# FoX queries and keys computed token-major and turned through DVE squares and DRAM, with the heads queued later

## The chip, the cores and the metric

The kernel runs on one core of one Trainium2 chip. The metric is the device time of one execution in microseconds; the time before is the median of 3 runs. The profile is one further execution, recorded by the hardware profiler. PE is the matrix engine (PEld its weight loads), DVE the vector engine, ACT the scalar engine, POOL and SP the two others, which here mostly issue DMAs.

## The reference

Two layers over 256 tokens of width 2048, each an adaLN-modulated norm, a mixer, a gated residual, then a norm, a SwiGLU FFN of width 5632 and a gated residual. Layer 0 mixes with an mLSTM, layer 1 with FoX attention, 16 heads of 128, which is where the change lies:

```python
def fox_mixer(h, w_in, b_f, w_out):
    proj = h @ w_in
    q, k, v, fl = jnp.split(proj, [D_MODEL, 2 * D_MODEL, 3 * D_MODEL], axis=-1)
    ...
    log_f = jax.nn.log_sigmoid(fl + b_f).transpose(0, 2, 1)
    o = forgetting_attention(heads(q), heads(k), heads(v), log_f)   # causal softmax, bias cum[t] - cum[s]
    return o.transpose(0, 2, 1, 3).reshape(B, T, D_MODEL) @ w_out
```

All is float32.

## The kernel before

**Products.** Float32 accuracy comes from split operands: each operand is kept as a high part (fp32r) and a low part (the remainder), and three products are summed: high by high, high by low, low by high. Weights are read by SP as tiles of four k-tiles by 512 columns, 1 MB each (`fetch`, line 250, from a pool of 5 buffers named raw). `split` (line 255) makes hi on ACT (line 261) and lo on DVE (line 262), two k-tiles at a time, in a pool of 4 pairs, so two weight tiles ahead at most. The normed activations hT (and y, the heads' outputs) hold high and low parts side by side, 512 wide for 256 tokens.

**Two forms of a projection.** `group_a` (line 316) has the activations as stationary and the weights as moving operand: per k-tile, for each of 2 token tiles, three matmuls of 512 columns (lines 288 to 290). It fills 2 PSUM banks with tokens in the partitions (token-major). `group_b` (line 296) has the weights as stationary operand: per k-tile, for each of 4 column tiles, a matmul of 512 moving columns (high weights by both parts of hT, line 271) and one of 256 (low weights by the high part, line 274). It fills 4 banks with columns in the partitions, as the heads want q and k; `total` (line 366) adds the two halves of a bank by an ACT copy and a DVE add. PSUM has 6 banks for projections and 2 (aux) for all else.

**Column steps.** After each weight tile a projection calls `tick` (line 245): it runs the next `adv` pieces of the list `steps`, makes waiting gate rows, and then adds `bgn` of credit for background work. Each whole credit issues one tile of the adaLN modulation (`ada_tile`, line 189): a 1 MB load on SP into the same raw buffers and one DVE instruction of 2.29 us on it. In FoX the credit is 0.66 a step. A clean step is 24 matmuls in `group_a`, 32 in `group_b`. `drain()` with no count runs all that is left in `steps` at once.

**The FoX stage** (lines 1276 to 1306). The first 512 columns of v come first, then the gates, then a loop over i = 0 to 3: q for heads 4i to 4i+3 (512 columns, four steps), k for the same, `drain()`, and then the twelve pieces of these four heads go into `steps`, interleaved over four: four `scores`, four `flip`, four `mix`. `scores` makes the logits on PE (lines 691, 696, 1229), the maximum on DVE (1239), the exponential on ACT (1244), the reciprocal and the scaling of the weights on DVE (1248, 1251). `flip` turns them on PE (958) and copies them (959). `mix` multiplies by v (1261, 1264) and splits the result into y (377, 378). The third value group is finished at i = 1, the fourth is made at i = 2 with two pieces a step; q and k run one piece a step. `project_out` (line 1093) multiplies y by the output weights in three groups of 512 columns and hands the fourth to `bridge`, which begins the FFN; the last four heads run two pieces a step in its first three steps, and the rest of them in a drain ahead of k-tile 12.

**The turn that exists.** The FFN already turns token-major data without PE for some of its groups: `blocks` (line 352) transposes 32x32 squares of a 128x512 tile on DVE (line 353) and writes the tile to a DRAM buffer named aside by POOL's DMA queue (line 357); `gather` (line 359) reads it back in four DMAs (line 361), so that columns stand in the partitions, with the four column tiles innermost; a strided ACT instruction (line 1171) makes it contiguous.

The program is written with a framework that lays out each engine's order and its waits at compile time, following the order of the code; SBUF buffers come from pools (16 slots of 4 KB a partition hold q, k, v, y and the heads' buffers).

Of the kernel before, what the change touches and what calls it, by code (L numbers as in the profile page):

```python
# [9 lines left out]
F32 = mybir.dt.float32  # L10
F32R = mybir.dt.float32r
BF16 = mybir.dt.bfloat16
AF = mybir.ActivationFunctionType
ALU = mybir.AluOpType
# [3 lines left out]
P = 128  # L18
T = 256
D = 2048  # L20
KT = D // P
# [10 lines left out]
def kernel(  # L32
# [5 lines left out]
    nc = tc.nc  # L38
# [13 lines left out]
    def nm(s):  # L52
        n_name[0] += 1
        return f"{s}_{n_name[0]}"

    def slot(dt=F32):
        return slots.tile([P, 1024], dt, tag="slot", name=nm("slot"))

    def bank():
        return psum.tile([P, 512], F32, tag="mm", name=nm("mm"))  # L60
# [4 lines left out]
    def t512():  # L65
        return tmp.tile([P, 512], F32, tag="t512", name=nm("t512"))

    def t256():
        return t512()[:, :T]
# [59 lines left out]
    for i, row in enumerate((crow, crow2)):  # L129
        for j in range(2):  # L130
            ps = bank()
# [100 lines left out]
    steps = []  # L232
# [6 lines left out]
    def drain(n=None):  # L239
        if steps:  # L240
            settle()
        for _ in range(len(steps) if n is None else min(n, len(steps))):
            steps.pop(0)()

    def tick(n, adv=1):
        drain(adv)
        grow_all()
        bg(n)
# [16 lines left out]
    def load_w(w, k0, nk, c0):  # L265
        raw = fetch(w, k0, nk, c0)
        return [p for j in range(0, nk, 2) for p in split(raw, j)]

    def mm_b(ps, hi, lo, rhs, first, last):
        def big():  # L270
            nc.tensor.matmul(ps, hi, rhs, start=first, stop=last, skip_group_check=True)  # L271

        def little():
            nc.tensor.matmul(  # L274
                ps[:, T:], lo, rhs[:, :T], start=False, stop=False, skip_group_check=True
            )

        if last:
            little()
            big()  # L280
        else:
            big()
            little()

    def mm_t(ps, hi, lo, act, t, first, last):
        a = act[:, t * P : (t + 1) * P]
        b = act[:, T + t * P : T + (t + 1) * P]
# [4 lines left out]
    def mm_a(ps, hi, lo, act, first, last):  # L292
        for t in range(2):
            mm_t(ps[t], hi, lo, act, t, first, last)

    def group_b(w, nk, c0, act, evac, bgn, adv=1):
        banks = [bank() for _ in range(4)]
        for k in range(0, nk, 4):
            ws = load_w(w, k, 4, c0)
            for m in range(4):  # L300
                cols = slice(m * P, (m + 1) * P)
                for j, (hi, lo) in enumerate(ws):
                    mm_b(
                        banks[m], hi[:, cols], lo[:, cols], act(k + j), k + j == 0, k + j == nk - 1
                    )
                if k + 4 == nk:
                    evac(m, banks[m])
            tick(bgn, adv)

    late = []  # L310

# [4 lines left out]
    def group_a(  # L316
        w, c0, act, bgn, adv=1, ka=0, kb=KT, row0=0, seed=None, banks=None, before=None, each=None,
        more=False,
    ):
        begun = banks is not None or seed is not None  # L320
        if banks is None:
            banks = [bank() for _ in range(2)]
        if seed is not None:
            for t in range(2):
                nc.scalar.copy(banks[t], seed[:, t, :])
        for k in range(ka, kb, 4):
            if before:
                before(k)
            ws = load_w(w, row0 + k, 4, c0)
            flush()  # L330
            if each:
                each(k)
            for j, (hi, lo) in enumerate(ws):
                mm_a(banks, hi, lo, act(k + j), not begun and k + j == ka, k + j == kb - 1 and not more)
            tick(bgn, adv)
        return banks
# [22 lines left out]
    def gather(whole, aside):  # L359
        for j in range(4):  # L360
            nc.gpsimd.dma_start(
                whole[32 * j : 32 * j + 32].rearrange("a (g b) m -> a g (b m)", b=32),
                aside.rearrange("t (i a) c -> a (t i) c", a=32)[:, :, j * P : (j + 1) * P],
            )

    def total(ps, out, scale=None):
        b = t256()
        nc.scalar.activation(b, ps[:, T:], AF.Copy, scale=1.0 if scale is None else scale)
        if scale is None:
            nc.vector.tensor_tensor(out, ps[:, :T], b, op=ALU.add)  # L370
        else:
            nc.vector.scalar_tensor_tensor(
                out=out, in0=ps[:, :T], scalar=scale, in1=b, op0=ALU.mult, op1=ALU.add
            )

    def split_act(src, dst):
# [365 lines left out]
    w = w_in  # L742
# [205 lines left out]
    def act_tile(lst, k):  # L948
        return lst[k // 2][:, k % 2, :]
# [101 lines left out]
    def interleave(*lists):  # L1051
        return [f for fs in zip(*lists) for f in fs]

    def keep_t(c0, bgn, scale=None, adv=1, layer_w=0):
        if layer_w == 0:
            i = COLS.index(c0)
            unit(i, start[i], KT, bgn)
            sp = SP[i]
            o = slot().rearrange("p (k t) -> p k t", t=T)

            def flip():
                for i in range(2):
                    nc.scalar.copy(o[:, 2 * i : 2 * i + 2, :], turned(sp, i))

            steps.append(flip)
            return o
        o = slot().rearrange("p (k t) -> p k t", t=T)
        group_b(w, KT, c0, h_act, lambda m, ps: total(ps, o[:, m, :], scale), bgn, adv)
        return o

    for i in range(1, 4):
# [20 lines left out]

    def project_out(wo, res, bgn, adv, upto, norm, w2, heads):
        act = lambda k: act_tile(y, k)
        for i in range(3):
            res.both(i, group_a(
                wo, 512 * i, act, bgn, adv, before=lambda k: drain() if k >= upto else None
            ))
        return bridge(wo, 0, KT, 1536, act, res, 3, norm, w2, heads)

# [118 lines left out]
    vals = {}  # L1219

    def fox_head(hd, q, k):
        st = {}

        def scores():
            S = abank()
            logits(u3, hd, S, False)
            for t in range(2):
                n = P * (t + 1)
                nc.tensor.matmul(  # L1229
                    S[:, T * t : T * t + n], q[:, t * P : (t + 1) * P], k[:, :n],  # L1230
                    start=False, stop=t == 1, skip_group_check=True,
                )
            mx = small([P, 2], "den", bufs=4)
            buf = slot()
            W = buf[:, : 3 * P]
            st["W"], st["WT"] = W, buf[:, 512 : 512 + 3 * P]
            sm = small([P, 2], "r", bufs=4)
            for t in range(2):
                nc.vector.tensor_reduce(
                    out=mx[:, t : t + 1], in_=S[:, slice(*causal[t])], axis=AX.X, op=ALU.max,  # L1240
                    negate=True,
                )
            for t in range(2):
                nc.scalar.activation(
                    W[:, slice(*packed[t])], S[:, slice(*causal[t])], AF.Exp,
                    bias=mx[:, t : t + 1], accum_out=sm[:, t : t + 1],
                )
            nc.vector.reciprocal(sm, sm)
            for t in range(2):
                wt = W[:, slice(*packed[t])]  # L1250
                nc.vector.tensor_scalar(wt, wt, sm[:, t : t + 1], None, op0=ALU.mult)

        def flip():
            weights_t(st["W"], st["WT"])

        def mix():
            v, WT = vals[hd // 4][:, :, hd % 4 * P : (hd % 4 + 1) * P], st["WT"]
            if hd % 2 == 0:
                y[hd // 2] = new_act()
            O = abank()  # L1260
            nc.tensor.matmul(
                O[:, :T], v[:, 0, :], WT[:, :T], start=True, stop=False, skip_group_check=True
            )
            nc.tensor.matmul(
                O[:, P:T], v[:, 1, :], WT[:, T:], start=False, stop=True, skip_group_check=True
            )
            split_act(O[:, :T], act_tile(y, hd))

        return [scores, flip, mix]

    def keep_v(banks):
        v = pair(slot())
        copy_a(v, banks)
        return v
# [17 lines left out]
    u3 = split3(cum, 16, new)  # L1292
    for i in range(4):
        if i == 1:
            vals[2] = keep_v(group_a(w, 2 * D + 1024, h_act, FR, ka=12, banks=begun[2 * D + 1024]))
        if i == 2:
            vals[3] = keep_v(group_a(w, 2 * D + 1536, h_act, FR, 2))
        q = keep_t(512 * i, FR, P ** -0.5, layer_w=1)
        k = keep_t(D + 512 * i, FR, layer_w=1)
        drain()  # L1300
        steps.extend(interleave(*[
            fox_head(4 * i + j, q[:, j, :], k[:, j, :]) for j in range(4)
        ]))
    res = Residual(1, G1, True)
    norm = Norm(res, 1, SC2, SH2)
    begun = project_out(fox_out, res, FR, 2, 12, norm, gate_up[1], [0, DFF, 512])
# [116 lines left out]
```

## Time and profile before

| what | value |
|---|---|
| median of 3 runs | 2279.05 us (2278.52 to 2279.84) |
| the profiled execution | 2279.4 us, span 2277.6 us |
| PE, DVE, ACT, POOL busy | 99%, 73%, 50%, 3% |
| granted TensorE clock | 0.999 |
| DMA | 640.69 MB, mean 281 GB/s |

A row of a group gives line, engine, operation, tiles (out<-in), count, then busy time and mean ns of one, then the idle time ahead of it and what ended that. A row of windows gives for a stretch the busy time of each engine with its count of instructions in brackets, then the granted clock, the busy share of the DMA engines and GB/s. A row of the timeline gives start, duration, engine, line and operation; rows of the same kind are merged (x2), and the idle time before the row stands in square brackets. A matmul's end is modelled and reaches into the next, so its pace is the distance between starts.

### The profile page before, as it was taken

The page shows a single profiled execution, that of the slowest core. Times are in us where ns is not written, and L with a number is a line of the kernel's source. Part 1 is how long each engine was busy: PE and PEld are TensorE (multiplying, and loading weights), DVE is VectorE, ACT ScalarE, POOL GpSimd, SP SyncE. Part 2 cuts the span into 40 slices and gives each one's busy share as a digit, 9 for nine tenths or more (in the row PEclk, how much of TensorE's full clock was granted, in tenths as well). Part 3 has the DMA queues.
Part 4 walks back from the last instruction along what each step waited for, and adds up shares of the span by engine and source line. Part 5 has one row for each costly group of instructions (what it writes and reads, how often), then busy time and mean ns, then how long its engine had stood idle before and what let it go on. Part 6 is the DMA issues. An engine that isn't in the chain of part 4 may idle for free.

```text
span 2277.6 us, 26530 instructions
## 1 busy us (share of the span) xinstructions
PE 2255.0 (99%) x10250; PEld 1848.2 (81%) x10250; DVE 1653.0 (73%) x1865; ACT 1139.6 (50%) x1493; POOL 71.2 (3%) x136
## 2 busy tenths in 40 slices
PE   8999999999999999999999999999999999999998
PEld 5877878888888888888888888887888888888886
DVE  7998789878887878875687777777665555555564
ACT  4778564555543344444555444455444443444443
POOL 1000000000000000100000000000100100010000
PEclk9999999999999999999999999999999999999999
DMA  9998989788888889996667877675777665566662
GB/s 394 371 369 321 353 307 354 283 338 334 325 335 330 326 335 349 360 350 219 217 238 288 299 273 277 250 274 189 271 276 255 221 204 189 201 223 219 206 233 98
DMA packets 93571, 640.69 MB, mean 281 GB/s; under 512 B 11443, under 2 KB 11891, under 8 KB 19077
## 3 DMA queue, kind: packets, MB, share of 16 engines
q1 hardware_dynamic: 86400, 617.79, 73.5%
q0 software_dynamic: 6896, 21.08, 3.1%
q8 instruction: 80, 1.31, 0.2%
q14 instruction: 47, 0.38, 0.0%
q10 hardware_dynamic: 148, 0.14, 0.0%
HBM read 628.44 MB, written 10.52 MB: 281 GB/s over the span
## 4 chain that ended last, share of the span: by engine, by line
PE 87%; DVE 5%; DMA 4%; ACT 2%; issue 1%; POOL 0%; SPq 0%; ACTq 0%; DVEq 0%; POOLq 0%
PE mm L289 25%; PE mm L290 25%; PE mm L288 25%; PE mm L271 5%; PE mm L274 3%; DMA ada<-in_ada_w_dram 3%; DVE lo L262 2%; DVE ada L193 2%; ACT hi L261 1%; DMA slot<-in_w_in_dram 1%; PE aux L1010 0%; PE aux L498 0%; PE aux L1229 0%; PE mm L569 0%; PE mm L565 0%
## 5 line engine op out<-in xcount | busy, mean ns | idle before, releaser
L262 DVE TENSOR_TENSOR lo<-raw,hi 128x1024 fp32r<-128x1024 f32 x764 | 924.2, 1221 | 470.8 <-ACT hi L261 469.5
L261 ACT CAST hi<-raw 128x1024 fp32r<-128x1024 f32 x764 | 796.9, 1054 | 870.7 <-PE mm L290 742.2
L289 PE MATMUL mm<-lo,hT 128*128 128x512 f32 x1846 | 720.3, 390 | 3.3 <-DVE lo L262 3.2
L290 PE MATMUL mm<-hi,hT 128*128 128x512 f32 x1846 | 719.8, 390 | 0.0
L288 PE MATMUL mm<-hi,hT 128*128 128x512 f32 x1846 | 719.1, 392 | 0.0
L193 DVE SCALAR_TENSOR_TENSOR ada<-ada,cs 128x2048 f32<-128x2048 f32 x192 | 438.7, 2285 | 55.7 <-DMA ada<-in_ada_w_dram 55.3
L289 PEld LDWEIGHTS mm<-lo,hT 128*128 128x128 f32 x1846 | 346.7, 188 | 78.5 <-DVE lo L262 7.4
L290 PEld LDWEIGHTS mm<-hi,hT 128*128 128x128 f32 x1846 | 346.5, 188 | 72.4 <-issue 0.5
L288 PEld LDWEIGHTS mm<-hi,hT 128*128 128x128 f32 x1846 | 346.5, 188 | 71.9 <-issue 0.5
L288 PE MATMUL mm<-hi,slot 128*128 128x512 f32 x960 | 375.0, 391 | 0.2 <-ACT slot L1043 0.2
L289 PE MATMUL mm<-lo,slot 128*128 128x512 f32 x960 | 374.2, 390 | 0.2 <-DVE lo L262 0.2
L290 PE MATMUL mm<-hi,slot 128*128 128x512 f32 x960 | 374.1, 390 | 0.0
L288 PEld LDWEIGHTS mm<-hi,slot 128*128 128x128 f32 x960 | 180.3, 188 | 38.0 <-ACT slot L1043 0.8
L290 PEld LDWEIGHTS mm<-hi,slot 128*128 128x128 f32 x960 | 180.2, 188 | 37.7 <-issue 0.7
L289 PEld LDWEIGHTS mm<-lo,slot 128*128 128x128 f32 x960 | 180.2, 188 | 37.5 <-DVE lo L262 0.6
L271 PE MATMUL mm<-hT,hi 128*128 128x512 f32 x512 | 181.5, 401 | 0.0
L274 PE MATMUL mm<-hT,lo 128*128 128x256 f32 x512 | 138.4, 281 | 0.4 <-DVE lo L262 0.4
L271 PEld LDWEIGHTS mm<-hT,hi 128*128 128x128 f32 x512 | 94.4, 188 | 19.6
L274 PEld LDWEIGHTS mm<-hT,lo 128*128 128x128 f32 x512 | 96.6, 189 | 4.1 <-DVE lo L262 1.1
L865 ACT ACTIVATE slot<-mm 128x512 f32<-128x512 f32 x78 | 45.3, 596 | 39.7 <-PE mm L290 37.9
L357 POOL DMA_DIRECT2D aside<-t x32 | 18.0, 562 | 1239.7 <-DVE t L353 1239.7
L1172 DVE TENSOR_TENSOR slot<-slot,slot 128x512 fp32r<-128x512 f32 x32 | 34.8, 1090 | 24.8 <-ACT slot L1171 24.8
(220 smaller groups left out, 1049.6 us busy)
## 6 DMA issues: line engine op xcount, KB each, us to landing
ada<-in_ada_w_dram SPq DMA_DIRECT2D x192, 1024.0 KB, 6.3
raw<-in_gate_up_dram SPq DMA_DIRECT2D x176, 1024.0 KB, 5.2
raw<-in_down_dram SPq DMA_DIRECT2D x88, 1024.0 KB, 4.9
raw<-in_fox_in_dram SPq DMA_DIRECT2D x48, 1024.0 KB, 4.9
raw<-in_w_in_dram SPq DMA_DIRECT2D x44, 1024.0 KB, 7.2
raw<-in_w_out_dram SPq DMA_DIRECT2D x16, 1024.0 KB, 5.8
raw<-in_fox_out_dram SPq DMA_DIRECT2D x16, 1024.0 KB, 4.9
aside<-t POOLq DMA_DIRECT2D x32, 256.0 KB, 2.5
```

What stands on the lines that cost most here:

```text
L193: nc.vector.scalar_tensor_tensor(out=raw, in0=raw, scalar=1.0, in1=cs, op0=ALU.mult, op1=ALU.mult, accum_out=acc[layer][:, j : j + 1],)
L261: nc.scalar.copy(hi, raw[:, j : j + 2, :])
L262: nc.vector.tensor_tensor(lo, raw[:, j : j + 2, :], hi.bitcast(F32), op=ALU.subtract)
L271: nc.tensor.matmul(ps, hi, rhs, start=first, stop=last, skip_group_check=True)
L274: nc.tensor.matmul(ps[:, T:], lo, rhs[:, :T], start=False, stop=False, skip_group_check=True)
L288: nc.tensor.matmul(ps, a, hi, start=first, stop=False, skip_group_check=True)
L289: nc.tensor.matmul(ps, a, lo, start=False, stop=False, skip_group_check=True)
L290: nc.tensor.matmul(ps, b, hi, start=False, stop=last, skip_group_check=True)
L357: nc.gpsimd.dma_start(aside, dst)
L865: nc.scalar.activation(SP[i][:, t, :], banks[t], func)
L1172: nc.vector.tensor_tensor(dst[:, :, T:], ps, dst[:, :, :T].bitcast(F32), op=ALU.subtract)
```

## The change

`group_b`, `mm_b` and `total` go. A FoX q or k group is now computed by `group_a`, evicted by two ACT copies (with the scale for q), turned by `blocks` and `gather`, and made contiguous by one ACT copy of 128x1024. A counter of steps, `clock`, is added, and a list `timed`, whose entries `tick` runs when their step has come: the contiguous copy five steps after its group (four for the last k), and the queueing of a block of heads one step after the copy of its k. The twelve pieces of a block are interleaved in two pairs (scores, scores, flip, flip, mix, mix, and again), two a step everywhere. The fourth value group moves behind the last k. `project_out` does the first 12 k-tiles of its first two groups ahead of the drain, and their last four after it.

```diff
     def tick(n, adv=1):
+        clock[0] += 1
+        while timed and timed[0][0] <= clock[0]:
+            timed.pop(0)[1]()
         drain(adv)
...
-        o = slot().rearrange("p (k t) -> p k t", t=T)
-        group_b(w, KT, c0, h_act, lambda m, ps: total(ps, o[:, m, :], scale), bgn, adv)
+        banks = group_a(w, c0, h_act, bgn, adv)
+        whole = slot().rearrange("p (t m) -> p t m", m=4)
+        aside = dram.tile([2, P, 512], F32, tag="aside", name=nm("aside"))
+        for t in range(2):
+            own = t512()
+            nc.scalar.activation(own, banks[t], AF.Copy, scale=1.0 if scale is None else scale)
+            blocks(t512(), own, aside[t])
+        gather(whole, aside)
+        o = slot().rearrange("p (m t) -> p m t", t=T)
+        timed.append((
+            clock[0] + LAND, lambda: nc.scalar.copy(o, whole.rearrange("p t m -> p m t"))
+        ))
         return o
...
         act = lambda k: act_tile(y, k)
+        first = {}
+        if upto == 12:
+            for i in range(2):
+                first[i] = group_a(wo, 512 * i, act, bgn, adv, kb=upto, more=True)
+            assert not timed
+            drain()
         for i in range(3):
             res.both(i, group_a(
-                wo, 512 * i, act, bgn, adv, before=lambda k: drain() if k >= upto else None
+                wo, 512 * i, act, bgn, adv, ka=upto if i in first else 0, banks=first.get(i),
+                before=lambda k: drain() if k >= upto else None,
             ))
...
     for i in range(4):
         if i == 1:
-            vals[2] = keep_v(group_a(w, 2 * D + 1024, h_act, FR, ka=12, banks=begun[2 * D + 1024]))
-        if i == 2:
-            vals[3] = keep_v(group_a(w, 2 * D + 1536, h_act, FR, 2))
-        q = keep_t(512 * i, FR, P ** -0.5, layer_w=1)
-        k = keep_t(D + 512 * i, FR, layer_w=1)
-        drain()
-        steps.extend(interleave(*[
-            fox_head(4 * i + j, q[:, j, :], k[:, j, :]) for j in range(4)
-        ]))
+            vals[2] = keep_v(
+                group_a(w, 2 * D + 1024, h_act, FR, 2, ka=12, banks=begun[2 * D + 1024])
+            )
+        q = keep_t(512 * i, FR, P ** -0.5, 2, layer_w=1)
+        if i == 3:
+            LAND = 4
+        k = keep_t(D + 512 * i, FR, None, 2, layer_w=1)
+        heads = [fox_head(4 * i + j, q[:, j, :], k[:, j, :]) for j in range(4)]
+        timed.append((clock[0] + LAND + 1, lambda hs=heads: steps.extend(
+            interleave(*hs[:2]) + interleave(*hs[2:])
+        )))
+    vals[3] = keep_v(group_a(w, 2 * D + 1536, h_act, FR, 2))
```

More of the change, by code (lines that the diff above doesn't have):

```diff
@@ L243, in drain @@
             steps.pop(0)()
+    clock = [0]
+    timed = []
     def tick(n, adv=1):
+        clock[0] += 1
+        while timed and timed[0][0] <= clock[0]:
+            timed.pop(0)[1]()
         drain(adv)
@@ L267, in load_w @@
         return [p for j in range(0, nk, 2) for p in split(raw, j)]
[L269 to L283, printed above, removed]
     def mm_t(ps, hi, lo, act, t, first, last):
@@ L294, in mm_a @@
             mm_t(ps[t], hi, lo, act, t, first, last)
[L296 to L308, printed above, removed]
     late = []
@@ L363, in gather @@
                 aside.rearrange("t (i a) c -> a (t i) c", a=32)[:, :, j * P : (j + 1) * P],
[L364 to L373, printed above, removed]
             )
@@ L1052, in interleave @@
         return [f for fs in zip(*lists) for f in fs]
+    LAND = 5
     def keep_t(c0, bgn, scale=None, adv=1, layer_w=0):
```

## The prediction

> **What bounds the kernel now.** I read the page first (busy shares, chain, costliest groups), then windows over the FoX stage, then PE's timeline in that stage.
>
> ```profile
> span 2277.6 us, 26530 instructions
> ...
> PE 2255.0 (99%) x10250; PEld 1848.2 (81%) x10250; DVE 1653.0 (73%) x1865; ACT 1139.6 (50%) x1493; POOL 71.2 (3%) x136
> ...
> PE 87%; DVE 5%; DMA 4%; ACT 2%; issue 1%; POOL 0%; SPq 0%; ACTq 0%; DVEq 0%; POOLq 0%
> ...
> L271 PE MATMUL mm<-hT,hi 128*128 128x512 f32 x512 | 181.5, 401 | 0.0
> ...
> L274 PE MATMUL mm<-hT,lo 128*128 128x256 f32 x512 | 138.4, 281 | 0.4 <-DVE lo L262 0.4
> ```
>
> PE is busy 99% of the span and makes 87% of the chain that ended last, so only shorter PE work, or a PE stall gained or lost, moves the time. The change deletes L271 and L274: 1024 matmuls, all of the q and k projections of FoX. Their busy times overlap, because matmuls are pipelined, so what they cost must be read from start to start. I cut the stage into column steps, each a weight tile of four k-tiles by 512 columns.
>
> ```profile
> core 0: us, PE busy (x) PEld busy (x) DVE busy (x) ACT busy (x) POOL busy (x), PEclk, DMA share, GB/s
> ...
> 1215.15:1261.23 46.08, 45.65 (x258) 39.19 (x256) 34.37 (x45) 23.02 (x32) 0.00 (x0) 1.00 0.73 270
> 1371.51:1399.84 28.33, 28.33 (x164) 24.48 (x162) 20.84 (x24) 11.40 (x16) 0.00 (x0) 1.00 0.80 287
> 1267.49:1273.23 5.74, 5.74 (x34) 4.94 (x33) 3.69 (x8) 4.21 (x9) 0.00 (x0) 1.00 1.01 400
> 1293.21:1298.85 5.64, 5.64 (x36) 4.95 (x35) 4.11 (x6) 2.39 (x5) 0.00 (x0) 1.00 0.85 289
> 1352.62:1358.36 5.74, 5.74 (x36) 4.99 (x35) 3.96 (x4) 1.71 (x3) 0.00 (x0) 1.00 0.97 388
> ```
>
> The first window is q and k of i = 0: 8 steps of 32 matmuls (x258 counts neighbours that reach over the edges), no head beside them. The second is 5 such steps. The last three are one step each: the first after a score, then after a flip, then after a mix. The form to come already runs in this stage for the value columns:
>
> ```profile
> start us, us, engine line op out<-in xcount [idle before <-releaser]
> ...
> 1326.64 0.58 PE L288 MATMUL mm<-hi,hT 128*128 128x512 f32 x1
> ...
> 1327.52 0.39 PE L288 MATMUL mm<-hi,hT 128*128 128x512 f32 x1
> ...
> 1331.60 0.39 PE L288 MATMUL mm<-hi,hT 128*128 128x512 f32 x1
> ...
> 1332.28 0.39 PE L691 MATMUL aux<-u,sel 96*128 96x512 bf16 x1
> ...
> 1340.30 0.48 PE L288 MATMUL mm<-hi,hT 128*128 128x512 f32 x1
> ...
> 1345.84 0.82 PE L958 MATMUL aux<-ident,slot 128*128 128x128 f32 x6
> ```
>
> From 1327.52 to 1331.60 lie 18 matmuls, 0.2267 us each, so a clean step of 24 takes 5.44 us. The step after scores takes 5.64 (1326.64 to 1332.28), the one after flips 5.54 (1340.30 to 1345.84).
>
> **The change, part by part. The projections.** Per k-tile the old form streams four times 512 + 256 columns in 8 matmuls, the new one six times 512 in 6: the same 3072 columns, a quarter fewer instructions. Without a head the old step takes (46.08 + 28.33 - 0.75) / 13 = 5.67 us; the 0.75 is a stall treated next. Against 5.44 this is 0.23 saved, 13 times: 3.0 us. Beside heads the rows give 5.74 against 5.64 after a score and 5.64 against 5.54 after a flip, so 0.10; after a mix I have only the old 5.74 and estimate 0.2. Over the 19 steps beside heads that is about 2.3 us. Sum 5.3 us less; bounds 4.4 (0.1 on half of the 13 steps too) and 6.0. The heads' own matmuls, 48 pieces, stay as they are and only move.
>
> By rows an instruction therefore costs a fixed part besides its columns: a pair of 512 and 256 takes 5.67 / 16 = 0.354 us (0.349 beside heads, 5.58 / 16), so 256 columns take 0.122 to 0.127, and twice that less 0.2267 leaves 0.018 to 0.028 us; times 256 fewer matmuls, 4.6 to 7 us, which agrees with the sum. [...]
>
> **The one stall of the old steps.**
>
> ```profile
> 1246.24 2.29 DVE L193 SCALAR_TENSOR_TENSOR ada<-ada,cs 128x2048 f32<-128x2048 f32 x1 [3.62 <-DMA ada<-in_ada_w_dram]
> ...
> 1249.06 0.40 PE L271 MATMUL mm<-hT,hi 128*128 128x512 f32 x1
> 1249.73 0.39 PE L274 MATMUL mm<-hT,lo 128*128 128x256 f32 x1 [0.27 <-DVE lo L262]
> ```
>
> DVE stood 3.62 us before a background ada tile that had not landed; lo came late behind it; PE lost 0.67 - 0.24 = 0.43 here and some 0.3 at the next pair. Nothing in the change removes this, so I count 0, with a bound of 0.75 gained.
>
> **Evictions and the turn.**
>
> ```profile
> L865 ACT ACTIVATE slot<-mm 128x512 f32<-128x512 f32 x78 | 45.3, 596 | 39.7 <-PE mm L290 37.9
> ...
> L1171 ACT CAST slot<-slot 128x512 fp32r<-128x512 f32 x32 | 35.7, 1118 | 19.9 <-DMA slot<-aside 19.9
> ...
> L353 DVE STREAM_TRANSPOSE t<-slot 128x512 f32<-128x512 f32 x32 | 31.8, 1066 | 0.0
> ...
> L368 ACT ACTIVATE t<-mm 128x256 f32<-128x256 f32 x32 | 12.2, 383 | 17.5 <-PE mm L271 17.5
> ...
> L370 DVE TENSOR_TENSOR slot<-mm,t 128x256 f32<-128x256 f32 x16 | 6.5, 419 | 2.5 <-ACT t L368 2.5
> L372 DVE SCALAR_TENSOR_TENSOR slot<-mm,t 128x256 f32<-128x256 f32 x16 | 6.4, 417 | 0.9 <-ACT t L368 0.7
> ```
>
> Removed: 12.2 us on ACT, 12.9 on DVE. Added on ACT: 16 evictions of 596 ns, and 8 strided copies of 128x1024, which I take as two of L1171, 2.24 us each: 27.4 us. Added on DVE: 16 transposes of 1066 ns, 17.1 us. So ACT gets 15 us more and DVE 4 us, none of it on PE's path as long as hi and lo come in time. What the cover is worth:
>
> ```profile
> 880.00:1000.00 120.00, 119.93 (x529) 98.80 (x528) 103.56 (x100) 55.16 (x56) 8.07 (x14) 1.00 0.97 364
> ...
> 1216.00:1444.00 228.00, 227.56 (x1278) 195.03 (x1277) 171.97 (x240) 110.10 (x185) 0.00 (x0) 1.00 0.77 280
> ```
>
> FoX would go from 172 to 176 us of DVE and from 110 to 125 of ACT in some 223 us: 79% and 56%. In 880 to 1000, layer 0's FFN, the same transposes and trips through DRAM run with DVE at 86%, DMA share 0.97, 364 GB/s, and PE is busy 119.93 of 120. So I count 0. If that cover were gone, each us that lo is late on all 32 steps would cost as many us.
>
> **The trip and its waits.** Each of the 8 groups writes 2 x 256 KB and reads 4 x 128 KB on POOL's queue, which is empty in this stage (x0). SP's queue gets nothing new; it only finds the engines fuller. The gather waits on POOL for the write; the copy waits on ACT for the gather, and behind the copy stand the hi casts and the heads' exps, for which DVE's lo and then PE wait.
>
> ```profile
> 908.03 2.00 DVE L353 STREAM_TRANSPOSE t<-slot 128x512 f32<-128x512 f32 x2
> ...
> 916.46 1.76 POOL L361 DMA_DIRECT2D slot<-aside  x3 [5.57 <-DMA aside<-t]
> ...
> 929.18 1.12 ACT L1171 CAST slot<-slot 128x512 fp32r<-128x512 f32 x1
> ```
>
> In the FFN the turned data is used 21.2 us after the first transpose. Here the copy is queued five steps after its group, 5 x 5.44 = 27.2 us or more, and for the last k four steps, 21.8 us and the heads between them. I count 0; the bounds are 0 and the rival below. The copy's own 2.24 us delays a hi cast, which has two steps of hi and lo buffers ahead of it.
>
> **The heads.** The changed schedule runs two pieces a step in pairs: a pair's flips come one step after its scores, where before they came two steps after. The chain scores, max, exp, reciprocal, scale must end within that step.
>
> ```profile
> 1332.19 0.54 DVE L1251 TENSOR_SCALAR slot<-slot,r 128x128 f32<-128x128 f32 x2
> ...
> 1340.64 0.54 DVE L1251 TENSOR_SCALAR slot<-slot,r 128x128 f32<-128x128 f32 x2
> ```
>
> The score pieces that end at 1326.64 would have flips at 1326.64 + 5.44 = 1332.1; their second head is scaled at 1332.7, 0.6 late. Those that end at 1334.08 would have them at 1339.5 and are scaled at 1341.2, 1.7 late, behind another ada tile. Bounds for 8 pairs: 0 (other matmuls are put ahead of the flips) and 8 x 1.15 = 9 us. I take 0.9, near zero: all that PE waited for from 1180 to 1560 is two lines, and L1251 is not among them, although the heads' pieces follow L1251 there too.
>
> ```profile
> PE aux L498 <- DVE slot L487: 1.6, 1, 1.6
> PE mm L274 <- DVE lo L262: 0.4, 2, 0.3
> ```
>
> Drains in one block go:
>
> ```profile
> 1470.06 0.47 PE L289 MATMUL mm<-lo,slot 128*128 128x512 f32 x1
> 1470.49 0.70 PE L1261 MATMUL aux<-slot,slot 128*128 128x256 f32 x2
> ```
>
> Here a mix stood behind its flip's copy, 0.43 - 0.23 = 0.2 us. The new order spreads the last heads over ten steps: 0.2 gained, bound 0.6. The value columns and the first 12 k-tiles of two output groups only change places, with their weight loads on SP; the number of steps, and so of background tiles, is the same.
>
> **Sum.** -5.3 + 0 + 0 - 0.2 + 0.9 = -4.6 us. The profiled execution took 2279.4 us, span 2277.6 and 1.8 around it: 2274.8. The median of the runs, 2279.05, is 0.35 below the profiled one, so 2274.5.
>
> **The rivals.**
>
> *A larger gain.* The projections reach 6.0, the 0.75 stall is not met again, the block drain gives 0.6, the flips cost nothing: 7.3, so 2271.7. For it: PE's waits are down to those two lines. Chance 0.15.
>
> *Part of it given back.* DVE meets unlanded ada tiles more often, since 8 MB more move in a stage that has no-head steps as short as the FFN's, and flips wait: 3 to 4 us lost, 2277.5 to 2278.5, no change that can be told. For it: the stall at 1249 at only 270 GB/s, and the 1.7 above. Against: PE at 119.93 of 120 in the FFN. Chance 0.22.
>
> *The fixed price per matmul is not what is saved.* [...] Against: 0.2267 at 1327 to 1331 in the same stage. Chance 0.07.
>
> *Slower: the gather lands after the copy is reached.* ACT then stands in front of the hi casts. The FFN's 21.2 us leave 6 us to the five steps, and the buffers ahead some 5 more, so it decides from landings about 11 us later than in the FFN; at 13 us, each of 8 copies would cost PE 2 us, 16 less the 4.6: 2290. For it: the windows above reach 400 GB/s and share 1.01 in single steps. Against: the FFN's landings are already those at 364 GB/s. Chance 0.08.
>
> **How the numbers follow.** My forecast has 0.48, and it lies on the bound of 0.2% (4.56 us, about what a measurement of this kernel can tell from no change), so half of it and a little over counts as faster. Faster: 0.15 + 0.31 = 0.46; same: 0.17 + 0.22 + 0.07 = 0.46; slower 0.08. The range takes in the larger gain with the 1 us beyond it, and the part given back, 2270.5 to 2278.5; the slower rival and most of the flips' upper bound (up to 2283) lie outside.
>
> **What would show it.** L271 and L274 gone, L288 to L290 in their place with 0.227 us from start to start and clean steps of 5.44 us; ACT's wait of the new copy on slot<-aside near zero; PE waits on DVE scaling or on lo below 2 us in the stage. It is wrong if the copy's wait is several us each, if PE's waits on lo grow to some us, or if the new steps take 5.6 us without a head.

## The result: slower by 1%

The changed kernel takes 2301.31 us (median of 5 runs, 2297.93 to 2305.32) against 2279.3 before (5 runs): ratio 1.0097, 95% interval 1.0082 to 1.0113. The forecast was 2274.5, range 2270.5 to 2278.5. The profiled execution, the fastest of the five, took 2297.93 us, 18.5 more than that of before. The page after, its span, busy shares, chain and the row of the background tiles:

```profile
span 2296.1 us, 26118 instructions
...
PE 2257.5 (98%) x9994; PEld 1839.8 (80%) x9994; DVE 1654.3 (72%) x1849; ACT 1153.7 (50%) x1485; POOL 99.0 (4%) x184
...
PE mm L279 12%; PE mm L280 12%; PE mm L278 11%; DMA ada<-in_ada_w_dram 4%; DVE lo L268 0%; DMA slot<-aside 0%; DMA aside<-t 0%; DVE ada L193 0%; PE aux L464 0%; PE mm L535 0%; PE mm L531 0%; PE mm L532 0%; PE aux L1214 0%; DVE t L329 0%; PE aux L1246 0%
...
L193 DVE SCALAR_TENSOR_TENSOR ada<-ada,cs 128x2048 f32<-128x2048 f32 x192 | 438.7, 2285 | 83.4 <-DMA ada<-in_ada_w_dram 82.9
```

PE, which bounded the kernel, now stands idle for 38.6 us (2296.1 less 2257.5), where it was 22.6. DVE waited 55.3 us for background tiles in the whole kernel before; now 82.9. What PE waited for in the FoX stage (1180 to 1600 us), in total, times and longest:

```profile
PE aux L924 <- DVE slot L1236: 12.5, 6, 5.3
PE mm L279 <- DVE lo L268: 3.1, 2, 2.3
PE mm L278 <- ACT hi L267: 2.1, 1, 2.1
```

17.7 us, where it was 0.4 plus the 1.6 at the bridge (2.0 in all). L924 is the flip (L958 before), L1236 the scaling of a head's weights. The windows of the changed kernel (busy per engine, clock, DMA share, GB/s) show a second loss:

```profile
1420.00:1436.00 16.00, 10.67 (x42) 8.42 (x41) 7.64 (x14) 4.98 (x12) 1.14 (x2) 0.79 0.91 279
...
1215.00:1533.00 318.00, 300.28 (x1349) 243.71 (x1348) 225.37 (x296) 158.29 (x238) 27.86 (x48) 0.97 0.80 282
```

The granted clock falls to 0.79 in this stretch. PE's and DVE's timelines there:

```profile
1423.87 0.40 PE L279 MATMUL mm<-lo,hT 128*128 128x512 f32 x1
1429.60 0.87 PE L924 MATMUL aux<-ident,slot 128*128 128x128 f32 x3 [5.33 <-DVE slot L1236]
...
1430.70 0.63 PE L278 MATMUL mm<-hi,hT 128*128 128x512 f32 x1
1431.13 0.63 PE L279 MATMUL mm<-lo,hT 128*128 128x512 f32 x1
```

```profile
1420.91 0.41 DVE L1224 TENSOR_REDUCE den<-aux 128x1 f32<-128x256 f32 x1
1425.76 2.29 DVE L193 SCALAR_TENSOR_TENSOR ada<-ada,cs 128x2048 f32<-128x2048 f32 x1 [4.44 <-DMA ada<-in_ada_w_dram]
...
1429.17 0.54 DVE L1236 TENSOR_SCALAR slot<-slot,r 128x128 f32<-128x128 f32 x2
```

DVE had the maxima of the pair's second head at 1421.3, but next in its order was a background tile that had not landed. It stood 4.44 us, worked on the tile 2.29, made a lo, and scaled the head at 1429.2. PE's flip waited 5.33 us for that. Afterwards two matmuls start 0.43 us apart, not 0.227: the clock is halved for a while. Four such halvings, 17.1 us in all, lie in the stage; before there was none. By the clock records of this trace three of the four last 3.41 us (from 1263.29, 1287.19 and 1454.44) and one 6.83 (from 1427.13). Each begins in a gap between matmul starts or within 1.2 us of its end: gaps of 2.73, 2.46 and 2.46 us for the three, of 5.73 for the one. There is no sharp bound: a gap of 2.45 us at the start of this kernel (23.39 to 25.85) and one of 2.00 us (1367.12 to 1369.12) were not followed by a halving.

Why the tiles were late: median time from issue to landing in 1215 to 1450 us (KB each, us), after and then before:

```profile
raw<-in_fox_in_dram SPq DMA_DIRECT2D x31, 1024.0 KB, 6.9
ada<-in_ada_w_dram SPq DMA_DIRECT2D x23, 1024.0 KB, 6.6
...
slot<-aside POOLq DMA_DIRECT2D x32, 128.0 KB, 7.7
```

```profile
raw<-in_fox_in_dram SPq DMA_DIRECT2D x31, 1024.0 KB, 4.8
ada<-in_ada_w_dram SPq DMA_DIRECT2D x25, 1024.0 KB, 4.9
```

The worst case of the changed kernel, on the queues of SP and POOL and on DVE:

```profile
1247.13 0.33 SPq L192 DMA_DIRECT2D ada<-in_ada_w_dram  x1
...
1247.85 2.34 POOL L337 DMA_DIRECT2D slot<-aside  x4 [5.45 <-PE mm L280]
...
1259.98 2.29 DVE L193 SCALAR_TENSOR_TENSOR ada<-ada,cs 128x2048 f32<-128x2048 f32 x1 [7.60 <-DMA ada<-in_ada_w_dram]
```

The tile is issued at 1247.1, four gathers follow on POOL, and it lands 12.8 us later. Lo stands behind it (PE waits 2.3 us), and so do the squares of k; this group's gather comes late as well, and ACT meets it:

```profile
1283.15 2.00 ACT L1045 COPY slot<-slot 128x1024 f32<-128x1024 f32 x1 [8.86 <-DMA slot<-aside]
```

Behind that copy stood a hi cast, and PE waited 2.1 us. That is the prediction's slower rival, but once, not eight times.

The gain is there, too. From 1418.53 to 1421.93 in the changed kernel lie 15 matmuls, 0.2267 us each:

```profile
1418.53 0.39 PE L278 MATMUL mm<-hi,hT 128*128 128x512 f32 x1
...
1421.93 0.39 PE L278 MATMUL mm<-hi,hT 128*128 128x512 f32 x1
```

### The profile page after: what moved, and what is told of

The parts are those of the page before. It is cut to its first block, busy times and chain, and to the rows that moved or that the text cites. A ratio compares the mean times of both kernels' runs of the same rounds, so it can differ in the third digit from the quotient of the medians.

```text
span 2296.1 us, 26118 instructions
## 1 busy us (share of the span) xinstructions
PE 2257.5 (98%) x9994; PEld 1839.8 (80%) x9994; DVE 1654.3 (72%) x1849; ACT 1153.7 (50%) x1485; POOL 99.0 (4%) x184
## 5 line engine op out<-in xcount | busy, mean ns | idle before, releaser
L279 PE MATMUL mm<-lo,hT 128*128 128x512 f32 x2102 | 823.3, 392 | 6.9 <-DVE lo L268 6.9
L278 PE MATMUL mm<-hi,hT 128*128 128x512 f32 x2102 | 822.7, 393 | 2.1 <-ACT hi L267 2.1
L280 PE MATMUL mm<-hi,hT 128*128 128x512 f32 x2102 | 822.2, 391 | 0.0
L193 DVE SCALAR_TENSOR_TENSOR ada<-ada,cs 128x2048 f32<-128x2048 f32 x192 | 438.7, 2285 | 83.4 <-DMA ada<-in_ada_w_dram 82.9
L279 PEld LDWEIGHTS mm<-lo,hT 128*128 128x128 f32 x2102 | 396.2, 188 | 93.2 <-DVE lo L268 11.4
L278 PEld LDWEIGHTS mm<-hi,hT 128*128 128x128 f32 x2102 | 396.0, 188 | 84.5 <-ACT hi L267 2.5
L280 PEld LDWEIGHTS mm<-hi,hT 128*128 128x128 f32 x2102 | 396.4, 189 | 82.9 <-issue 0.5
L333 POOL DMA_DIRECT2D aside<-t x48 | 27.0, 563 | 1189.6 <-DVE t L329 1142.4
L337 POOL DMA_DIRECT2D slot<-aside x96 | 56.3, 593 | 109.1 <-DMA aside<-t 83.4
L1156 ACT CAST slot<-slot 128x512 fp32r<-128x512 f32 x32 | 35.5, 1111 | 19.0 <-DMA slot<-aside 19.0
L414 ACT ACTIVATE t<-X 128x512 f32<-128x512 f32 x32 | 20.2, 630 | 39.3 <-DVE X L409 39.3
L409 DVE TENSOR_TENSOR X<-X,t 128x512 f32<-128x512 f32 x48 | 32.3, 686 | 0.5
```

The costliest lines, as they stand in the source:

```text
L193: nc.vector.scalar_tensor_tensor(out=raw, in0=raw, scalar=1.0, in1=cs, op0=ALU.mult, op1=ALU.mult, accum_out=acc[layer][:, j : j + 1],)
L278: nc.tensor.matmul(ps, a, hi, start=first, stop=False, skip_group_check=True)
L279: nc.tensor.matmul(ps, a, lo, start=False, stop=False, skip_group_check=True)
L280: nc.tensor.matmul(ps, b, hi, start=False, stop=last, skip_group_check=True)
L333: nc.gpsimd.dma_start(aside, dst)
L337: nc.gpsimd.dma_start(whole[32 * j : 32 * j + 32].rearrange("a (g b) m -> a g (b m)", b=32), aside.rearrange("t (i a) c -> a (t i) c", a=3 ...
```

## The experiments

Theory A: the trips through DRAM make tiles land late, DVE stands in order before them, and PE waits for what is behind. Theory B: the order of the heads in pairs is the cost, the trip is harmless. Each comparison is with the kernel before on the same chip (its medians 2278.6 to 2280.5). Of each edit only the main lines are shown.

### Order and trip, apart and together

```diff
 e_four
-            interleave(*hs[:2]) + interleave(*hs[2:])
+            interleave(*hs)
 e_notrip (e_four_notrip has both edits)
-            blocks(t512(), own, aside[t])
-        gather(whole, aside)
+            nc.vector.transpose(                       # flat is the tile whole is a view of
+                flat[:, 512 * t : 512 * t + 512].rearrange("p (j b m) -> p j m b", j=4, m=4),
+                own.rearrange("p (m j b) -> p j m b", m=4, j=4),
+            )
 e_heads_alone: the kernel before with tick, project_out and the FoX loop of the change,
 keep_t with group_b as it was
```

e_four: 

> The changed kernel with the twelve pieces of a block interleaved over all four heads again (four scores, four flips, four mixes, two pieces a step), so that a flip comes two steps after its scores; the trip through DRAM stays. Theory A (late tiles: the trips make the background tiles and weights land late, DVE stands in order before them, and what is queued behind is late): the flips get slack, but the waits on lo and hi at the start of the stage (5 us, and the half-clock time after them) stay; about 2283 to 2290. Theory B (the pair order: flips one step after their scores are what costs, the trip is harmless): PE's 12.5 us on the scaling and most of the half-clock time go; about 2274 to 2279.

2294.42 us, ratio 1.0063 (1.0046 to 1.0080). Its PE waits in the stage:

```profile
PE mm L279 <- DVE lo L268: 5.5, 5, 1.8
PE mm L278 <- ACT hi L267: 3.8, 1, 3.8
PE aux L924 <- ACT slot L1229: 2.3, 2, 1.6
PE aux L657 <- ACT slot L1229: 2.2, 3, 1.0
```

The waits on the scaling went, others came, and DVE's wait for background tiles in the stage went from 45.9 to 55.8 us. The time lies above the ranges of both theories, so A had the size wrong too; theory B falls as the main cause.

e_notrip: 

> The changed kernel without the trip through DRAM: DVE's squares go straight into the tile that the ACT copy reads, so aside and the gathers of q and k (8 MB) are left out, and q and k are only turned within squares of 32; all else, the pair order too, stays. Theory A: background tiles land as before (4.9 us median), DVE's wait for them falls from 46 to about 23 us, PE's waits fall to 1 to 5 us; 2273 to 2280. Theory B: the flips still wait some 12 us; 2290 to 2298.

2277.16 us, ratio 0.9986 (0.9976 to 0.9996), PE's wait on the scaling 2.8 us. Theory A's range.

e_four_notrip: 

> Both of the others together: four-way order and no trip (q and k again only turned within squares). Both theories: no PE wait in the stage beyond 1 us, so what is left is the gain of the projections, 4.4 to 6 us on the kernel before; 2273 to 2276. If it stays above 2279 there is a third cost (ACT copies, DVE squares).

2272.28 us, ratio 0.9966 (0.9953 to 0.9979): 7.4 us faster than before (by the interval 4.8 to 10.7), somewhat more than either theory gave. PE is busy 314.89 of 315 us in the stage:

```profile
1215.00:1530.00 315.00, 314.89 (x1455) 259.25 (x1454) 243.43 (x314) 173.04 (x258) 0.00 (x0) 1.00 0.76 279
```

The squares and the copies are in this kernel, so their 4 us on DVE and 15 on ACT cost nothing. Without the trip the turn of q and k stays unfinished, so this is a bound for the gain and no kernel to use.

e_heads_alone: 

> The kernel before with the changed order of the heads alone: pairs, two pieces a step, queued six steps behind their k, fourth value group last, output groups begun ahead of the drain; projections in the old form, without squares, trip or copies. Theory A: little or no loss, 2278 to 2284. Theory B: the flips wait as in the changed kernel, 12 us and half-clock time; 2290 to 2300.

2280.48 us, ratio 1.0001 (0.9991 to 1.0010). The new order costs nothing with the old projections; with the new ones it costs 2277.16 - 2272.28 = 4.9 us. The trip costs 24 us with pairs (2301.31 - 2277.16, from different sets of runs) and 22 with four (2294.42 - 2272.28).

### What of the trip costs

```diff
 e_four_unused: squares into flat, written to aside from there, gathered into a slot nobody reads
+            blocks(flat[:, 512 * t : 512 * t + 512], own, aside[t])
+        gather(slot().rearrange("p (t m) -> p t m", m=4), aside)
 e_four_write: the same without the gather line
 e_four_flatread: aside written as before, and in place of gather
+            nc.gpsimd.dma_start(flat[:, 512 * t : 512 * t + 512], aside[t])
 e_four_swap: runs of 512 bytes on the write, one read
+            nc.gpsimd.dma_start(                       # for i in range(4)
+                aside[:, t, i, :].rearrange("(j a) c -> a j c", a=32),
+                dst[32 * i : 32 * i + 32].rearrange("a (j c) -> a j c", j=4))
+        nc.gpsimd.dma_start(flat, aside.rearrange("p t i c -> p (t i c)"))
 e_four_actq: gather by nc.scalar, two steps after the group
```

e_four_unused: 

> Four-way order, the whole trip through DRAM (16 writes and 32 gathers), but the ACT copy reads DVE's squares directly, so nothing waits for a gather (q and k only turned within squares of 32; the gathered tile is not used). Theory A1 (the trip's packets make SP's loads land late, and DVE's in-order wait for a background tile hands that on): as with the trip in use, 2288 to 2296, DVE's wait for background tiles near 50 us. Theory A2 (ACT standing on the copy until the gather lands, in front of the hi casts, is the cost): as without the trip, 2272 to 2276.

2294.75 us, ratio 1.0068 (1.0053 to 1.0083), as with the trip in use. ACT's wait for the gather is not the cost (A2 falls). DVE's wait for background tiles is longer still:

```profile
DVE ada L193 <- DMA ada<-in_ada_w_dram: 67.1, 24, 7.3
```

e_four_write: 

> Four-way order, only the 16 writes to DRAM (4 MB), no gathers; the ACT copy reads DVE's squares directly (q and k only turned within squares). If bytes alone count, half of the trip's cost of about 22 us: near 2283. If it is the gathers and their short rows, near 2273. If it is the writes, near 2292. Theory A2: 2272 to 2276.

2275.38 us, ratio 0.9982 (0.9973 to 0.9992). The writes cost some 3 us, which the two intervals hardly tell from nothing, the reads back 19.

e_four_flatread: 

> Four-way order, writes as in the changed kernel, and the four gathers replaced by two plain reads of 256 KB in rows of 2 KB, so the same bytes come back in another order (q and k are only turned within squares). Theories S1 and S2: 2274 to 2279, next to the 2275.4 with writes alone. Theory R: 2288 to 2297.

2290.92 us, ratio 1.0045 (1.0030 to 1.0060): reading back costs without short rows as well (theory R), 15.5 us over the writes alone.

e_four_swap: 

> Four-way order and a trip that carries the same data with its short rows on the other side: the writes are cut into runs of 512 bytes (8 DMAs of 64 KB a group), laid down so that one DMA of 512 KB reads 4 KB a partition in one run. The result is the reference's. Theory S1 (short rows cost only where they are read): 2273 to 2278. Theory S2 (short rows cost on either side) or theory R (reading back 512 KB a group costs, whatever the rows): 2288 to 2297.

2282.29 us, ratio 1.0017 (1.0007 to 1.0026), between the ranges: one read of 512 KB in rows of 4 KB, with the writes cut up, disturbs less than two or four, and the longest landing of a load in the stage is 8.4 us, where it is 12.8 with the gathers (the profiled execution, 2278.96 us, is the fastest of its ten). Of the versions that keep the trip in use and all of the work it is the fastest, but no faster than the kernel before.

e_four_actq: 

> Four-way order and the whole trip in use, the four gathers issued from ACT's hardware queue two steps after their group in place of POOL's. The result is the reference's. Theory Q (POOL's software-made queue is what disturbs SP's loads): 2274 to 2279. Theories S1, S2 and R (the gathers' transfers themselves): 2288 to 2297.

2292.79 us, ratio 1.0057 (1.0042 to 1.0072). That is next to e_four's 2294.42: POOL's queue is not the cause.

### How the late tiles reach PE

```diff
 e_four_late: ada_op is the DVE instruction of ada_tile, put off by one tile in the FoX loop
+                behind[0].append((layer, v, k, raw))
+                catch_up(1)
 e_four_slow
-    ... fr=0.66
+    ... fr=0.58
 e_four_noada: want(1, SC2, SH2) and want(1, G2) become constants
 e_notrip_ring4 (on e_four_notrip)
-    rawp = ctx.enter_context(tc.tile_pool(name="rawp", bufs=5))
+    rawp = ctx.enter_context(tc.tile_pool(name="rawp", bufs=4))
 e_four_loads: ada_tile returns after its load for those 48 tiles
 e_four_ops: ada_tile has no load for them, and DVE works on cs in place of raw
```

e_four_late: 

> Four-way order and the whole trip in use, as in the changed kernel; in the FoX loop a background tile's DVE instruction is put one tile later than its load, so that DVE reaches it 1 to 2 steps after the load was queued. Theory A1, with DVE's in-order wait as the channel: that wait falls from 56 us to under 15 us, and with it PE's waits; 2274 to 2282. If the weights' own lateness is the channel (the tile holds a raw buffer longer, so loads start later): 2290 or more. Theory A2: as the four-way order with the trip, 2290 to 2297.

2296.91 us, ratio 1.0080 (1.0063 to 1.0096). No help, and the time lies in the range that was given for late weights as the channel. DVE's wait stayed at 60.5 us. But the edit did not give the tiles more time. From the issue of a tile's load to the moment DVE had ended what stood before the tile, the trace has a median of 5.0 us in 1215 to 1440, where e_four has 4.9. So the run says little about the channel. That a tile held longer makes the next load start later, since SP waits for the same five buffers, is a reading of the code and not shown.

e_four_slow: 

> Four-way order and the whole trip in use, with the background credit in FoX at 0.58 instead of 0.66 a step (33 tiles instead of 38 from the stage's start to its end; the rest move into the FFN behind). Theory A1: fewer loads compete, the trip's cost of 22 us falls by a third or more, 2278 to 2288. Theory A2: unchanged, 2290 to 2297.

2297.3 us, ratio 1.0079 (1.0064 to 1.0094). A miss: fewer tiles, the same loss; ACT stood on one copy 13.7 us, and DVE's wait for tiles was 68.3 us.

e_four_noada: 

> Four-way order and the whole trip in use, without the 48 background tiles of layer 1's FFN modulation (their loads and DVE instructions are left out and the modulation is set to a constant, so the output is not the reference's); 38 of them lay in this stage. Theory L (the reads back cost because the five raw buffers and DVE are already near their limit with weights and background tiles): PE's waits in the stage go, 2269 to 2275. Theory D (the reads back themselves delay the weights, whoever else loads): 2285 or more, with PE's waits on lo and hi still there.

2269.88 us, ratio 0.9957 (0.9942 to 0.9972), PE busy without a gap, with the trip in use (POOL x48):

```profile
1215.00:1530.00 315.00, 315.00 (x1456) 259.43 (x1455) 180.50 (x244) 174.31 (x258) 27.76 (x48) 1.00 0.60 205
```

So the trip costs only together with background tiles. Theory D falls.

e_notrip_ring4: 

> Four-way order without the trip (q and k only turned within squares), and one raw buffer fewer, 4 in place of 5. Theory L: with one load fewer in flight the stage loses as with late landings although nothing reads back; DVE's wait for tiles in the stage above 50 us, PE's waits 5 us or more there, and other stages with many loads lose too; 2290 to 2330. Theory D: the stage stays as with 5 buffers, PE's waits under 2 us there; 2272 to 2280.

2283.04 us, ratio 1.0011 (1.0002 to 1.0021), and this stage loses nothing; the loss lies in other stages:

```profile
1215.00:1530.00 315.00, 315.00 (x1457) 259.56 (x1456) 243.82 (x316) 171.80 (x258) 0.00 (x0) 1.00 0.77 280
```

A smaller number of buffers alone is not it, so of theory L only the part on the background tiles holds. DVE's waits for tiles summed to 40.4 us there, but the longest was 3.8 us. Over all the runs it is this longest wait that goes with the loss: at most 4.5 us in the stage wherever the median is under 2290 us, 4.8 to 7.9 us wherever it is over.

e_four_loads: 

> Four-way order and the whole trip in use; the 48 background tiles of layer 1's FFN modulation are still loaded by SP into the raw buffers, but DVE's instruction on them is left out (the modulation is a constant, so the output is not the reference's). Theory W (DVE standing in order before a background tile that has not landed, with all else queued behind, is the channel): as without those tiles, 2268 to 2274. Theory C (the loads compete with the weights, so that weights land late): as with the tiles, 2288 to 2296, PE's waits on lo and hi.

2274.53 us, ratio 0.9975 (0.9965 to 0.9984). The loads still land late (weights 6.4 us median, 10.9 at most), but no DVE instruction stands before a tile, and PE waits 2.5 us in the stage. Theory W: of the 22 us, some 20 need DVE's instruction behind the load. Part of that may be its 2.29 us of work each, which this run leaves out as well, and part that a tile's buffer, which nobody reads here, is free as soon as the tile has landed.

e_four_ops: 

> Four-way order and the whole trip in use; the same 48 tiles are not loaded, and DVE runs its 2.29 us instruction on data that already lies in SBUF (the modulation is wrong, so the output is not the reference's). Both theories: no late tile to wait for and no loads to compete, 2268 to 2274. If it is 2285 or more, DVE's busy time itself is the cost.

2287.2 us, ratio 1.0030 (1.0019 to 1.0042). That is the "2285 or more" of the expectation, but it does not answer the question: the 48 instructions, which have no load to wait for, ran nearly all ahead of the FoX stage. DVE has no more to do in the stage than without the tiles, PE is busy throughout, and the loss lies before it, where PE is busy 601.94 of 615 us:

```profile
1215.00:1530.00 315.00, 315.00 (x1457) 259.61 (x1456) 181.69 (x245) 172.80 (x254) 27.84 (x48) 1.00 0.59 198
...
600.00:1215.00 615.00, 601.94 (x2668) 496.36 (x2667) 543.10 (x566) 270.26 (x307) 22.76 (x39) 0.99 0.79 290
```

From 1140 to 1168 us DVE runs these instructions between the small ones of the norm ahead of FoX, and PE waits there 9.2 us, in two stalls, for the norm's line 459. So DVE's work on the tiles, without any late load, can cost PE where it stands in the way; whether it would in FoX, tied to its place, stays open.

## Why the prediction was wrong, step by step

**The projections.** The gain was right in size as far as the runs can tell: 5.3 us forecast, and 7.4 (4.8 to 10.7) measured where all else was taken away, with the vanished block drain of 0.2 and the stall of 0.75 in it. The third rival, whose chance was counted as no change, is out in its outcome: the new form runs at 227 ns from start to start in this stage, and the 7.4 us are a gain. But the fixed part of 18 to 28 ns per matmul is not what the starts show either. In clean steps the old form's matmuls of 256 columns take 117 ns to the next start and those of 512 columns 236; the new form's take 227 (1216 to 1244 us, before and e_four_notrip). Twice 117 less 227 leaves 7 ns, which is 1.8 us over 256 matmuls. The larger part of the gain is that a matmul of 512 columns took 9 ns longer in the old form. Why it did stays open.

**The squares, copies and evictions**, counted at 0: right (e_four_notrip).

**The trip, counted at 0:** the step that failed. It rested on the FFN, where the same trips ran at a DMA share of 0.97 with PE at 119.93 of 120. Two things were missed. The first is DVE's lead. In FoX there is one trip in four steps, in the FFN one in eight, and with the trips the median landing of tiles in FoX went from 4.9 to 6.6 us. But late landings alone are not it: in the FFN the tiles land later still, and DVE hardly waits for them. Where DVE sat idle before a background tile (us, times) and how long the tiles took to land, before in 880 to 1000, before and after in 1215 to 1440:

```profile
  DMA ada<-in_ada_w_dram: 5.3, 1
...
DMA to landing us min/median/max: 6.9/7.8/11.9
```

```profile
  DMA ada<-in_ada_w_dram: 21.7, 15
...
DMA to landing us min/median/max: 4.7/4.9/6.6
```

```profile
  DMA ada<-in_ada_w_dram: 42.0, 16
...
DMA to landing us min/median/max: 4.7/6.2/12.8
```

By the trace, a tile of the FFN has a median of 10.6 us from the issue of its load until DVE has ended what stands before it; in FoX it has 4.8 us (5.2 in the changed kernel). So in FoX DVE already came to 15 of 24 tiles before they had landed, and no reserve was left for a longer landing. The second is what stands behind a tile on DVE: in the FFN lo, the products, the squares and the low parts of the turned data (L262, L1155, L353, L1172), in FoX also the heads' maxima and scales, which PE needs a step later. The prediction named "part of it given back" for this, at 3 to 4 us; it was 24.

**The flips, 0.9 of 0 to 9 us:** the size failed. PE waited 12.5 us on the scaling in the profile. The order alone is worth 0 (old projections) to 4.9 us (new ones, no trip); the rest is the trip's lateness in the same chain. That PE waited for nothing on that line before was no sign of slack for the new order: there the flips came two steps after their scores, here one.

**The slower rival**, the copy on ACT, was the wrong mechanism for the right side: with no copy waiting for a gather the time is the same (2294.75 against 2294.42).

**Not in the sum at all:** PE's clock. The halvings cover 17.1 us; 2.9 of them fell into idle time, so about 14.2 / 2 = 7 us were lost by matmuls at half speed. 17.7 + 7 less the 2.0 of before and a gain of 6 to 7 gives 16 to 17 us, next to the 18.5 between the two profiles; some 2 us are not accounted for.

What stays open is how much of the loss is DVE's standing and how much its work on the tiles, why a read back delays other loads so much more than a write of the same size (median landing of background tiles in 1215 to 1440: 6.7 us in e_four_unused, 5.5 in e_four_write, 5.2 in e_four_notrip), and why two reads of 256 KB do more than one of 512 KB (2290.92 against 2282.29 us, the writes cut up in the latter).

## What to carry to other kernels

A cover that holds in one stage is only evidence for another if the loads have the same lead there and the same things are queued behind them (here a median of 10.6 us of lead in the FFN, 4.8 in FoX): ask how long before its use each load is issued, what stands behind each wait on an engine (here a head that PE needed stood behind 4.44 us of DVE's wait for a tile), and how soon PE needs it. A spill and reload that is off the path can still lengthen other loads' landings, as here from 6.6 us to 12.8 at the longest; check the longest landing times against the lead of whatever waits for them. A PE stall can cost more than its length: here gaps between matmul starts of 2.46 to 5.73 us came with 3.41 to 6.83 us at half the clock. Look at the granted clock behind each stall.

## What the runs showed of the hardware

With equal columns, 32 matmuls of 512 and 256 columns take 5.67 us (236 and 117 ns from start to start) where 24 of 512 take 5.44 (227 ns each). Beside the background tiles, reading 4 MB back from DRAM in the stage cost 19 us in gathers of 128 KB and 15.5 us in plain reads of 256 KB, while writing 4 MB cost some 3 us; without those tiles the whole trip cost nothing that can be told (2269.88 us). Three of the four clock halvings of the changed kernel's FoX stage lasted 3.41 us each, the one at the longest gap 6.83; two of them followed gaps of 2.46 us between matmul starts, and a gap of 2.45 us elsewhere in the same execution was followed by none.
